# A hybrid attention and convolution layer on eight cores: projection stage reordered with staged weights and dead keys left out, finalize work of a unit spread, tail begun inside the last attention unit

## The chip, the cores and the metric

The kernel runs on all 8 cores of one Trainium2 chip. Times are device microseconds (us) of the slowest core. In the profile, PE is the tensor engine, ACT the ScalarE, DVE the VectorE, POOL the GpSimd and SP the SyncE that issues most loads.

## The reference, cut to what matters

```python
h = rmsnorm(x, mix_norm_g)                       # x: (4, 4096, 1024)
q, k, v, g_attn, cb, cc, ch, g_conv = split(h @ w_in)      # each 512 columns
# A: 4 heads of differential attention with bias -slope_h * |t - s|; slopes 1/4, 1/16, 1/64, 1/256
probs = softmax(q1 k1^T / 8 + bias) - lam * softmax(q2 k2^T / 8 + bias)
o_A   = rmsnorm(probs @ v, subln_g) * (1 - lambda_init) * silu(g_attn)
# B: short gated convolution of width 3
o_B   = cb * conv3(cc * ch) * silu(g_conv)
x = x + concat(o_A, o_B) @ w_out                 # "y" below is this product
gate = sigmoid(rmsnorm(x, ple_norm_g) @ w_ple_gate)
x = x + gate * (p @ w_ple_proj)
return rmsnorm(x, final_norm_g)
```

Each core owns 2048 of the 4096 rows of one sequence (the near half). For attention it also needs k and v of the other 2048 rows (the far half), and computes them itself.

## The kernel before

It has three stages: projections with the gate and the convolution; attention in 16 units (4 heads, 4 query chunks of 512 rows each); and a tail over 16 tiles of 128 rows.

**Projections.** A pipeline normalises 32 row tiles. The k and v weights come by software DMA, which casts them to bf16 on the way. The near half is done in three passes: q with the norm, then k, then v. Every k and q group also has its squares summed over the partitions by one matmul against a matrix of ones, followed by a VectorE maximum. That gives the bound that is subtracted in the exponential.

```python
load_w(0, [(512, 512, 0)])                       # k weights, software DMA with cast
load_w(1, [(1024, 512, 0)])                      # v weights
for s in range(32 + LAG):
    # ... (norm pipelines np_a, np_b; late constants; load of the q weights)
    if 0 <= m < 16:                              # far half
        k_chunk(0, r, j, SO, rdy)                # 8 matmuls of 512 columns
        v_tile(1, 4 * j + r, 16 + 4 * j + r, rdy)
    elif 16 <= m < 32:
        q_chunk(2, r, j, rdy)                    # near half, pass 1
# ...
for tokc in range(4):
    for h in range(NH):
        k_chunk(0, h, tokc, 0, rdy_all)          # near half, pass 2
# ...
for tl in range(16):
    v_tile(1, tl, tl, rdy_all)                   # near half, pass 3
```

**Attention.** For each key tile, two matmuls make the scores, ScalarE takes exponentials of 128x1024 elements, and two tiles later eight matmuls of 129 columns multiply by v. When a group of tiles ends, VectorE moves the accumulators out. When the unit ends, VectorE does the finalize work at once, in one piece:

```python
def finalize_part1(unit, h, qc, tks):            # cut: waits, operands
    reciprocal(rs); tensor_scalar(c2)
    for sb_ in range(4): tensor_scalar(OT[sb_])                 # VectorE
    for sb_ in range(4): scalar_tensor_tensor(OT[sb_])          # VectorE
    tensor_tensor(ON = OT * OT)                                 # VectorE
    tensor_reduce(ssq)                                          # VectorE
    # POOL: variance, power -1/2, ON = OT * rsd
    pending.append([12, part2])                  # transposes and product with the gate, 12 tiles later

for i in range(NT + 2):
    if i < NT: emit_S(i)                         # scores and exponential
    if i >= 2: emit_PV(i - 2)                    # product with v; evacuation; finalize_part1
    # ... run those of pending that have come due
```

**Tail.** The first y tile and 32 fp32 transposes of p follow the last unit, then a barrier, then a loop in stages over the 16 tiles:

```python
for it in range(NTILE + 4):                      # cut: bounds on it
    st_x1n(it - 1)                               # normalise
    st_c2a(it - 2)                               # tanh on ACT, two products on DVE
    st_load(it + 1); st_y(it)                    # 16 matmuls, residual add on DVE
    st_c1(it - 1)                                # transposes, 2 ACT copies, p and gate matmuls
    st_c2b(it - 2); st_sq3(it); st_d(it - 3)     # squares; output
```

Of the kernel before, what the change touches and what calls it, by code (L numbers as in the profile page):

```python
# [18 lines left out]
SLOPES = [2.0 ** (-8.0 * (h + 1) / NH) for h in range(NH)]  # L19
LAMBDA_INIT = 0.8 - 0.6 * 1.0  # L20
# [41 lines left out]
def build_program(debug=None):  # L62
# [6 lines left out]
    p_d = din("p", [SO, 256])  # L69
# [18 lines left out]
    with es:  # L88
# [39 lines left out]
        mx_all = sb("mx_all", [128, 48], F32)  # L128
        negM = sb("negM", [128, 1], F32)
# [17 lines left out]
        mq = sb("mq", [128, 2], F32)  # L147
        mk2 = sb("mk2", [128, 2], F32)
# [26 lines left out]
        for dst, src in [(gmix, gmix_d), (gple, gple_d), (subln, subln_d), (convw, convw_d), (lamv, lam_d)]:  # L175
            tkc = cslot.dma(SP, dst[:], src)
# [5 lines left out]
        POOL.eng.memset(mx_all[:], 0.0)  # L182
# [6 lines left out]
        def late_consts():  # L189
            DVE.need(tkc)  # L190
# [34 lines left out]
        SQB = [cv.take([128, 512], BF16) for _ in range(2)]  # L225
# [16 lines left out]
        with pes:  # L242
# [12 lines left out]
            wslot = [Slot(nc, es, "w%d" % i) for i in range(3)]  # L255
            w_free = [None, None, None]
# [3 lines left out]
            sqb_free = [None, None]  # L260
            mx_idx = [0]
            state = {"xt_free": [None] * NXT, "xn_free": [None, None], "nt": 0, "xt_gen": [0] * NXT,
# [3 lines left out]
            def flush_deferred():  # L266
                while deferred:
                    deferred.pop(0)()
# [9 lines left out]
            class NormPipe:  # L278
# [8 lines left out]
                def _emit_step(self, step):  # L287
# [10 lines left out]
                    if 0 <= i < self.n:  # L298
# [6 lines left out]
                        DVE.need(tk_sq[i])  # L305
                        tk_v[i] = DVE.mark(DVE.eng.tensor_scalar(out=v_all[:, k:k + 1], in0=ss_all[:, k:k + 1],  # L306
# [56 lines left out]
            def norm_bound(s, tk_mm):  # L363
                idx = mx_idx[0]
                mx_idx[0] += 1
                b = idx % 2
                ACT.need(tk_mm, sqb_free[b])
                t_sq = ACT.mark(ACT.eng.activation(out=SQB[b][:], in_=psP[s][:], func=AF.Square))

                def part_b():  # L370
                    PE.need(t_sq, psM_free[0])
                    t_m = PE.mark(PE.eng.matmul(psM[:], lhsT=ones_b[:], rhs=SQB[b][:], start=True, stop=True))  # L372
                    sqb_free[b] = t_m
                    DVE.need(t_m)
                    t_r = DVE.mark(DVE.eng.tensor_reduce(out=mx_all[:, idx:idx + 1], in_=psM[:], axis=AX.X, op=ALU.max))  # L375
                    psM_free[0] = t_r

                deferred.append(part_b)
                return t_sq

            def k_chunk(buf, h, tokc, tokbase, ready_tk):
                s, tk = proj_fm(buf, h * 128, tokc, ready_tk)
                ACT.need(tk)
                t_cp = ACT.mark(ACT.eng.activation(out=KT[:, h, tokbase + tokc * 512: tokbase + (tokc + 1) * 512], in_=psP[s][:],  # L384
                                                   func=AF.Copy))
                t_sq = norm_bound(s, tk)
                psP_free[s] = [t_cp, t_sq]

            def q_chunk(buf, h, tokc, ready_tk):
# [4 lines left out]
                t_sq = norm_bound(s, tk)  # L394
                psP_free[s] = [t_cp, t_sq]

            def v_tile(buf, tl, rglob, ready_tk):
# [3 lines left out]
                for c in range(8):  # L401
                    ins = PE.eng.matmul(psP[s][:], lhsT=HT[:, c, tl * 128:(tl + 1) * 128], rhs=WB[buf][:, c, :],  # L402
                                        start=(c == 0), stop=(c == 7))
                tk = PE.mark(ins)
                flush_deferred()
                DVE.need(tk, tk_pc)
                psP_free[s] = DVE.mark(DVE.eng.tensor_copy(out=VA[:, rglob, :, 0:128],
                                                           in_=psP[s][:].rearrange("p (h d) -> p h d", h=NH)))

            load_w(0, [(512, 512, 0)])  # L410
            load_w(1, [(1024, 512, 0)])
            ht_chunk_free = [None] * 4
            np_a = NormPipe(list(range(16, 32)), lambda i: i * 128, lambda i: None)
            np_b = NormPipe(list(range(0, 16)), lambda i: i * 128, lambda i: ht_chunk_free[i // 4])
            ev0 = np_a.advance(0)
            DVE.need(ev0)
            tk_hth = DVE.mark(DVE.eng.tensor_copy(out=HTH[:], in_=HT[:, :, 0:2]))
            LAG = 4
            for s in range(32 + LAG):
                if s < 16:  # L420
                    np_a.advance(s)
                elif s < 32:
                    np_b.advance(s - 16)
# [5 lines left out]
                if 0 <= m < 16:  # L429
                    j, r = m // 4, m % 4  # L430
                    rdy = np_a.advance(4 * j + 3)
                    k_chunk(0, r, j, SO, rdy)
                    v_tile(1, 4 * j + r, 16 + 4 * j + r, rdy)
                    if r == 3:
                        ht_chunk_free[j] = PE.last()
                elif 16 <= m < 32:
                    j, r = (m - 16) // 4, (m - 16) % 4
                    rdy = np_b.advance(4 * j + 3)
                    q_chunk(2, r, j, rdy)
            flush_deferred()  # L440
            rdy_all = np_b.advance(15)
            norm_done = [state["last_sq"], state["last_xn"], state["last_tr"]]
            w_free[2] = PE.last()
            load_w(2, [(1536, 512, 0)])
            for tokc in range(4):
                for h in range(NH):
                    k_chunk(0, h, tokc, 0, rdy_all)
            flush_deferred()
            w_free[0] = PE.last()
            DVE.need(DVE.last())  # L450
            nq = 16
            nk = 32
            t_a = DVE.mark(DVE.eng.tensor_reduce(out=mq[:, 0:1], in_=mx_all[:, 16:32], axis=AX.X, op=ALU.max))
            DVE.need(t_a)
            DVE.eng.tensor_reduce(out=mk2[:, 0:1], in_=mx_all[:, 0:16], axis=AX.X, op=ALU.max)
            t_b = DVE.mark(DVE.eng.tensor_reduce(out=mk2[:, 1:2], in_=mx_all[:, 32:48], axis=AX.X, op=ALU.max))
            DVE.need(t_b)
            t_c = DVE.mark(DVE.eng.tensor_tensor(out=mq[:, 1:2], in0=mk2[:, 0:1], in1=mk2[:, 1:2], op=ALU.max))
            DVE.need(t_c)
            t_d = DVE.mark(DVE.eng.tensor_tensor(out=mk2[:, 0:1], in0=mq[:, 0:1], in1=mq[:, 1:2], op=ALU.add))  # L460
            DVE.need(t_d)
            tk_negM = DVE.mark(DVE.eng.tensor_scalar(out=negM[:], in0=mk2[:, 0:1], scalar1=-1.0 / 16.0, scalar2=None, op0=ALU.mult))

            DVE.need(tk_negM, LC["t_io"])
            for h in range(NH):
                DVE.eng.tensor_scalar(out=biasA[:, h, :], in0=iotaA[:], scalar1=SLOPES[h], scalar2=negM[:], op0=ALU.mult, op1=ALU.add)
                DVE.mark(DVE.eng.tensor_scalar(out=biasB[:, h, :], in0=(iotaB0 if h == 0 else iotaB)[:], scalar1=-SLOPES[h], scalar2=negM[:], op0=ALU.mult, op1=ALU.add))

            def conv_blocks(cc):
                return [(2048 + cc * 128, 128, 0), (2560 + cc * 128, 128, 128), (3072 + cc * 128, 128, 256),  # L470
                        (3584 + cc * 128, 128, 384)]

            load_w(0, conv_blocks(0))
            for tl in range(16):
                v_tile(1, tl, tl, rdy_all)
            w_free[1] = PE.last()
            load_w(1, conv_blocks(1))
            th_free = [norm_done, norm_done]
            thi = [0]
            for tokc in range(4):  # L480
                for h in range(NH):
# [18 lines left out]
            for cc in range(4):  # L500
# [27 lines left out]
                for tokc in range(4):  # L528
# [16 lines left out]
                    DVE.need(tk_u[min(tokc + 1, 3)], tk_pad, tk_hl, ca_free[a], tkc)  # L545
# [57 lines left out]
        PF32 = rc1.take([128, 16, 256], F32)  # L603
        XT3 = [rc1.take([128, D], F32) for _ in range(2)]
        X1 = [rc1.take([128, D], F32) for _ in range(2)]
# [5 lines left out]
        X1NT = [rc3.take([128, 8, 128], BF16) for _ in range(2)]  # L611
# [14 lines left out]
        ppslot = [Slot(nc, es, "pld%d" % g) for g in range(4)]  # L626
        tk_pld = []
        P3 = {}

        def prefetch_phase3():  # L630
            SP.need(PE.last(), DVE.last())
            gslot.dma(SP, GFIN[:], gfin_d)
            P3["gfin"] = gslot.dma(SP, GPLEB[:], gpleb_d)
            for t_ in range(2):
                P3["ldx", t_] = x3slot[t_].dma(SP, XT3[t_][:], x_d[t_ * 128:(t_ + 1) * 128, :])
            for g in range(4):
                tk_pld.append(ppslot[g].dma(SP, PF32[:, 4 * g:4 * g + 4, :],
                                         p_d.rearrange("(t p) c -> p t c", p=128)[:, 4 * g:4 * g + 4, :]))
# [3 lines left out]
        for half_ in range(2):  # L642
            wt_slot.dma(POOL, WOUT[:, :, half_ * 512:(half_ + 1) * 512],
                        wout_d.rearrange("(c p) n -> p c n", p=128)[:, :, half_ * 512:(half_ + 1) * 512])
        for half_ in range(2):
            wt_slot.dma(POOL, WG[:, :, half_ * 512:(half_ + 1) * 512],
                        wg_d.rearrange("(c p) n -> p c n", p=128)[:, :, half_ * 512:(half_ + 1) * 512])
# [446 lines left out]
```

## Time and profile before

The time before is 963.74 us (median of 3 runs); with one more run on the chip that timed the change, 964.75 us of 4. The profiled execution lasted 961.9 us on its slowest core, core 5.

| stage (median over the 8 cores of the profile) | us |
|---|---|
| start to first projection group | 38.2 |
| start to first exponential (all projections, gate, convolution) | 362.2 |
| units 0 to 3 (head 0) | 56.2 |
| units 4 to 14 | 341.1 |
| unit 15 (the last) | 35.6 |
| last exponential to end (tail) | 164.4 |

I derived the stages from the first exponential of each unit in the trace. The next lines are from the page of the kernel before: part 1 (busy us, share, instructions per engine) and the clock row of part 2 (tenths of full speed, 40 equal slices).

```profile
PE 838.9 (87%) x6210; PEld 445.6 (46%) x6210; DVE 450.7 (47%) x814; ACT 584.3 (61%) x783; POOL 123.5 (13%) x155
...
PEclk9999999999999997888999999999999997999997
```

The tensor engine leads with 87%, but that is an average of stages with different limits. The windows view of core 5 separates them. Its columns are named in its first line: length, then busy us and instructions of each engine, granted clock, DMA share.

```profile
core 5: us, PE busy (x) PEld busy (x) DVE busy (x) ACT busy (x) POOL busy (x), PEclk, DMA share, GB/s
37.00:112.00 75.00, 68.94 (x398) 34.47 (x397) 50.00 (x83) 34.87 (x73) 15.75 (x23) 0.98 0.47 129
112.00:220.00 108.00, 97.06 (x507) 44.91 (x506) 57.38 (x95) 43.47 (x82) 13.71 (x14) 1.00 0.28 49
...
361.00:417.00 56.00, 40.73 (x314) 23.35 (x314) 35.84 (x86) 37.08 (x69) 11.66 (x15) 0.74 0.60 85
...
759.00:795.00 36.00, 32.07 (x335) 19.33 (x332) 8.92 (x23) 33.98 (x36) 2.24 (x3) 1.00 0.01 1
795.00:962.00 167.00, 145.27 (x748) 69.44 (x748) 108.83 (x128) 73.85 (x116) 34.18 (x35) 0.93 0.28 95
```

The far half (37 to 112) and the near half (112 to 220) are tensor work with gaps of 6 and 11 us. Head 0 (361 to 417) has no engine near full and a granted clock of 0.74. In the last unit (759 to 795) ScalarE is busiest with 33.98 us of 36, but the tensor engine follows at 32.07.

The pace of a full tile in that unit stands in the timeline of the tensor engine, core 5 (start us, duration us, engine, line, operation). The last line is from the ScalarE timeline of the same stretch; its bracket is the idle time ahead of it and what ended that.

```profile
769.54 0.37 PE L718 MATMUL psS<-QT,KT 64*128 64x512 bf16 x1
...
769.87 0.63 PE L805 MATMUL psBig<-VA,ARENA 128*128 128x129 bf16 x8
770.55 0.37 PE L718 MATMUL psS<-QT,KT 64*128 64x512 bf16 x1
...
771.88 0.39 PE L718 MATMUL psS<-QT,KT 64*128 64x512 bf16 x1
...
772.77 0.39 PE L718 MATMUL psS<-QT,KT 64*128 64x512 bf16 x1
...
762.25 16.26 ACT L737 ACTIVATE ARENA<-psS,biasB 128x1024 bf16<-128x1024 f32 x16 [0.57 <-PE psS L720]
```

One tile takes 770.55 - 769.54 = 1.01 us, and sixteen exponentials in a row take 16.26 us, 1.02 us each. This is ScalarE's pace. Where the tensor engine had to catch up (starts at 771.88, 772.77 and 773.66 in the same trace) it ran at 0.89 us per tile. So its slack is 1.01 - 0.89 = 0.12 us per tile, not more.

In head 0 the end of a unit looks like this on VectorE (timeline, core 5: start us, duration us, engine, line, operation):

```profile
379.37 0.69 DVE L759 TENSOR_TENSOR ARENA<-ARENA 128x512 f32<-128x512 f32 x1
380.17 0.69 DVE L761 TENSOR_REDUCE ssq<-ARENA 128x4 f32<-128x512 f32 x1
381.03 1.36 DVE L820 TENSOR_TENSOR ARENA<-psBig,fB 128x387 f32<-128x387 f32 x3 [0.17 <-DVE ssq L761]
```

The reduction of the finalize work ends and the next evacuation (L820) follows with 0.17 us of idle time.

In the tail, the chain of waits between 815 and 830 us is tensor work alone. The first line gives shares; each later line is one link: start us, us, what.

```profile
by line: PE psS L900 45.5%; PE psS L950 39.2%; PE psBig L941 11.5%; PE psBig L929 6.0%
...
819.54 3.59 PE psS L950 x16
823.12 3.45 PE psS L900 x16
826.58 0.45 PE psBig L929 x8
827.02 0.86 PE psBig L941 x4
```

L950 is the gate product, L900 the y product, L929 the transposes and L941 the p product. One tile costs about 8.4 us, and the tensor engine waits for nobody.

### The profile page before, as it was taken

The page shows a single profiled execution, that of the slowest core. Times are in us where ns is not written, and L with a number is a line of the kernel's source. Part 1 is how long each engine was busy: PE and PEld are TensorE (multiplying, and loading weights), DVE is VectorE, ACT ScalarE, POOL GpSimd, SP SyncE. Part 2 cuts the span into 40 slices and gives each one's busy share as a digit, 9 for nine tenths or more (in the row PEclk, how much of TensorE's full clock was granted, in tenths as well). Part 3 has the DMA queues.
Part 4 walks back from the last instruction along what each step waited for, and adds up shares of the span by engine and source line. Part 5 has one row for each costly group of instructions (what it writes and reads, how often), then busy time and mean ns, then how long its engine had stood idle before and what let it go on. Part 6 is the DMA issues. An engine that isn't in the chain of part 4 may idle for free.

```text
span 961.9 us, 17031 instructions; the slowest of 8 cores (956.1 to 961.9 us)
## 1 busy us (share of the span) xinstructions
PE 838.9 (87%) x6210; PEld 445.6 (46%) x6210; DVE 450.7 (47%) x814; ACT 584.3 (61%) x783; POOL 123.5 (13%) x155
## 2 busy tenths in 40 slices
PE   0688979999999996889889999899999897999993
PEld 0344434444444443445555555555555554444441
DVE  1577684343277667644432213312312313577775
ACT  2344554502211116779999999999999992455553
POOL 2221130011110002010000000000000001122222
PEclk9999999999999997888999999999999997999997
DMA  8763422055550006700000000000500000133332
GB/s 175 203 154 96 140 73 42 4 44 45 44 44 1 2 1 84 114 1 1 2 2 1 2 2 1 2 1 4 174 1 1 2 1 22 53 124 132 132 110 88
DMA packets 37920, 51.04 MB, mean 53 GB/s; under 512 B 18512, under 2 KB 29392, under 8 KB 37840
## 3 DMA queue, kind: packets, MB, share of 16 engines
q1 hardware_dynamic: 12336, 36.85, 12.0%
q0 software_dynamic: 25504, 13.11, 11.9%
q8 instruction: 52, 0.85, 0.4%
q14 instruction: 28, 0.23, 0.1%
HBM read 54.67 MB, written 8.39 MB: 66 GB/s over the span
## 4 chain that ended last, share of the span: by engine, by line
PE 61%; DVE 13%; ACT 12%; issue 8%; DMA 2%; POOL 2%; DVEq 0%; SPq 0%; ACTq 0%; POOLq 0%
PE psP L357 20%; PE psBig L805 16%; PE psS L718 11%; ACT ARENA L737 8%; PE psP L402 6%; DMA ARENA<-x 2%; PE psS L900 2%; PE psS L950 2%; POOL r L916 2%; DVE VA L961 2%; DVE VA L965 1%; DVE KT L904 1%; ACT SGA L911 1%; DVE psS L728 1%; PE psT L329 1%
## 5 line engine op out<-in xcount | busy, mean ns | idle before, releaser
L737 ACT ACTIVATE ARENA<-psS,biasB 128x1024 bf16<-128x1024 f32 (+3 forms) x292 | 264.2, 1007 | 14.7 <-PE psS L720 13.4
L805 PE MATMUL psBig<-VA,ARENA 128*128 128x129 bf16 x2904 | 254.7, 227 | 16.8 <-DVE ARENA L825 5.8
L357 PE MATMUL psP<-ARENA 128*128 128x512 bf16 x1024 | 232.3, 382 | 0.9 <-DVE ARENA L522 0.7
L805 PEld LDWEIGHTS psBig<-VA,ARENA 128*128 128x128 bf16 x2904 | 173.2, 100 | 110.0 <-issue 101.4
L718 PE MATMUL psS<-QT,KT 64*128 64x512 bf16 (+3 forms) x429 | 152.4, 355 | 35.3 <-ACT ARENA L737 23.7
L720 PE MATMUL psS<-QT,KT 64*128 64x512 bf16 (+3 forms) x429 | 156.4, 365 | 0.0
L357 PEld LDWEIGHTS psP<-ARENA 128*128 128x128 bf16 x1024 | 99.2, 98 | 117.1 <-issue 6.3
L737 ACT ACTIVATE ARENA<-psS,biasA 128x1024 bf16<-128x1024 f32 (+3 forms) x156 | 131.2, 896 | 25.8 <-DVE psS L728 18.1
L718 PEld LDWEIGHTS psS<-QT,KT 64*128 64x128 bf16 x429 | 39.9, 93 | 96.0 <-issue 84.6
L728 DVE SCALAR_TENSOR_TENSOR psS<-T_relu,psS 128x256 f32<-128x256 f32 x64 | 27.4, 427 | 90.9 <-PE psS L720 90.8
L329 PE MATMUL psT<-ident_b,ARENA 128*128 128x128 bf16 x256 | 22.2, 238 | 43.4 <-DVE ARENA L317 21.0
L950 PE MATMUL psS<-ARENA,QT 128*128 128x512 bf16 x256 | 58.4, 381 | 0.0
L402 PE MATMUL psP<-ARENA 128*128 128x512 bf16 x256 | 58.0, 379 | 0.0
L375 DVE TENSOR_REDUCE mx_all<-psM 128x1 f32<-128x512 f32 x48 | 33.1, 690 | 52.4 <-PE psM L372 51.0
L820 DVE TENSOR_TENSOR ARENA<-psBig,fB 128x387 f32<-128x387 f32 (+1 forms) x48 | 22.0, 509 | 67.8 <-PE psBig L805 67.1
L764 POOL TENSOR_SCALAR vsq<-ssq 128x4 f32<-128x4 f32 x16 | 3.1, 192 | 388.7 <-DVE ssq L761 388.7
L384 ACT ACTIVATE KT<-psP 128x512 bf16<-128x512 f32 x32 | 19.1, 596 | 52.0 <-PE psP L357 52.0
L781 DVE SCALAR_TENSOR_TENSOR ARENA<-psBig,sublns,SGA 128x512 bf16<-128x512 f32 x16 | 12.0, 751 | 81.1 <-PE psBig L777 81.1
L309 POOL TENSOR_TENSOR rstd_all<-v_all,mhalf 128x1 f32<-128x1 f32 x32 | 30.8, 964 | 105.5 <-DVE v_all L306 105.4
L825 DVE TENSOR_TENSOR ARENA<-psBig,ARENA 128x387 f32<-128x387 f32 (+1 forms) x48 | 22.3, 510 | 46.8 <-PE psBig L805 46.0
L329 PEld LDWEIGHTS psT<-ident_b,ARENA 128*128 128x128 bf16 x256 | 17.8, 106 | 52.2 <-issue 49.9
L302 ACT ACTIVATE ARENA<-ARENA 128x1024 bf16<-128x1024 f32 x32 | 33.8, 1057 | 10.8 <-DMA ARENA<-x 10.5
(111 smaller groups left out, 875.2 us busy)
## 6 DMA issues: line engine op xcount, KB each, us to landing
ARENA<-x SPq DMA_DIRECT2D x32, 512.0 KB, 3.8
KT<-x SPq DMA_DIRECT2D x16, 512.0 KB, 4.2
y<-VA SPq DMA_DIRECT2D x16, 512.0 KB, 2.9
ARENA<-w_in POOLq DMA_DIRECT2D x4, 1024.0 KB, 17.1
ARENA<-w_in POOLq DMA_DIRECT2D x16, 256.0 KB, 9.1
ARENA<-w_out POOLq DMA_DIRECT2D x2, 1024.0 KB, 13.1
ARENA<-w_g POOLq DMA_DIRECT2D x2, 1024.0 KB, 24.6
KT<-p SPq DMA_DIRECT2D x4, 512.0 KB, 12.4
```

The lines of the kernel that those rows point to most:

```text
L302: tk_sq[i] = ACT.mark(ACT.eng.activation(out=JUNK[:], in_=XT[s][:], func=AF.Square, accum_out=ss_all[:, k:k + 1]))
L309: tk_r[i] = POOL.mark(POOL.eng.tensor_tensor(out=rstd_all[:, k:k + 1], in0=v_all[:, k:k + 1], in1=mhalf[:], op=ALU.pow))
L329: ins = PE.eng.transpose(out=psT[s2][:, c * 128:(c + 1) * 128], in_=XN[s2][:, c * 128:(c + 1) * 128], identity=ident_b[:])
L357: ins = PE.eng.matmul(psP[s][:], lhsT=WB[buf][:, c, wcol0:wcol0 + 128], rhs=HT[:, c, tokc * 512:(tokc + 1) * 512], start=(c == 0), stop=(c ...
L375: t_r = DVE.mark(DVE.eng.tensor_reduce(out=mx_all[:, idx:idx + 1], in_=psM[:], axis=AX.X, op=ALU.max))
L402: ins = PE.eng.matmul(psP[s][:], lhsT=HT[:, c, tl * 128:(tl + 1) * 128], rhs=WB[buf][:, c, :], start=(c == 0), stop=(c == 7))
L718: PE.eng.matmul(psS[b][:, x0:x1], lhsT=KT[0:64, h, kt * 128:(kt + 1) * 128], rhs=QT[0:64, h, qc * 512 + x0:qc * 512 + x1], start=True, sto ...
L720: tk_s = PE.mark(PE.eng.matmul(psS[b][:, 512 + x0:512 + x1], lhsT=KT[64:128, h, kt * 128:(kt + 1) * 128], rhs=QT[64:128, h, qc * 512 + x0: ...
L728: tk_in = DVE.mark(DVE.eng.scalar_tensor_tensor(out=dgb, in0=T_relu[:].unsqueeze(1).to_broadcast([128, 2, 128]), scalar=-2.0 * SLOPES[h], ...
L737: ins = ACT.eng.activation(out=ET[e][:].rearrange("p (j q) -> p j q", j=2)[:, :, s0 * 128:s1 * 128], in_=ps3[:, :, s0 * 128:s1 * 128], fun ...
L805: ins = PE.eng.matmul(acc_region(r), lhsT=ET[e][:, j * 512 + sb_ * 128: j * 512 + (sb_ + 1) * 128], rhs=VA[:, kt, h, :], start=st_, stop=f ...
L950: ins = PE.eng.matmul(psG[:, half_ * 512:(half_ + 1) * 512], lhsT=X1NT[s][:, c, :], rhs=WG[:, c, half_ * 512:(half_ + 1) * 512], start=(c ...
```

## The change

The intent was to feed the tensor engine better in the projections, and to start the tail inside the last unit, where ScalarE sets the pace.

1. The k and v weights come as fp32 over the hardware queue, and ScalarE and GpSimd cast half of each.
2. Far keys whose bias makes the exponential zero are not projected: 4 k groups, and 17 quarters (one head in one tile) of the v tiles.
3. One norm pipeline instead of two. In the near half q, k and v of one chunk follow each other. Half of the v evacuations go to ScalarE, 4 small loads move later.
4. The bound takes four groups at a time: four matmuls of 32 output columns and one maximum instead of four.
5. The finalize work is cut into pieces that run 1, 2, 3, 4, 6 and 12 tiles after the unit, and its square moves to GpSimd.
6. Three y tiles, cut into 24 pieces of two matmuls, run inside the last unit, with their residual adds, squares and normalisation. p arrives transposed from the host. The barrier is gone, and the tail loop has a new order.

The diff holds smaller moves too. The bound is now one per head, and the tables made from it are built between the gate projections. The variance steps of the norms go from VectorE to GpSimd. The weights of the tail come one block at a time at the ends of units, and the last tail tile is handled in halves.

```diff
-load_w(0, [(512, 512, 0)])
-load_w(1, [(1024, 512, 0)])
+def stage_w(buf, c0, stg):                       # 2 loads on SP, fp32
+    # ...
+    def cast():                                  # ACT casts c 0:4, POOL casts c 4:8
+def k_dead(h, j):
+    return SLOPES[h] * (512 * j + 1) >= EXP_ZERO
+def v_h0(tl):
+    return next(h for h in range(NH) if SLOPES[h] * (128 * tl + 1) < EXP_ZERO)
 # ... near half
-        q_chunk(2, r, j, rdy)                    # then all k, then all v
+        for u_ in range(3 * r, 3 * r + 3):
+            if u_ < 4:   q_chunk(2, u_, j, rdy)
+            elif u_ < 8: k_chunk(0, u_ - 4, j, 0, rdy)
+            else:        v_tile(1, 4 * j + u_ - 8, 4 * j + u_ - 8, rdy)
 # ... bound
-    PE.eng.matmul(psM[:], lhsT=ones_b[:], rhs=SQB[b][:], start=True, stop=True)
+    for h in range(NH):
+        src = SQB[grp[h][0]][:] if h in grp else zb
+        PE.eng.matmul(psM[32 * h:32 * h + 32, :], lhsT=ones_b[:, 0:32], rhs=src, start=True, stop=True)
 # ... end of a unit
+for n_, fn in ((1, piece_a), (2, piece_b), (3, piece_c), (4, piece_d), (6, piece_e), (12, piece_f)):
+    pending.append([n_, fn, unit])               # piece_d: square on POOL; piece_e: reduction on DVE
 # ... attention loop
+    if i == first_u15 + 2:
+        for t_ in range(NPRO):                   # NPRO = 3
+            filler += list(y_pieces(t_))
+            if t_ == 0: filler.append(lambda: st_x1n(0))
+            if t_ == 1: filler.append(lambda: st_x1n(1)); filler.append(fill_tr0)
+    if filler: filler.pop(0)()                   # one piece per tile
 # ... tail loop (cut: bounds on it)
+for it in range(NTILE + 1):
+    st_x1n(it + 1)
+    st_g(it)
+    fr["psT3"] = st_tr(it + 1, psT3, fr["psT3"], ACT)   # transposes, two ACT copies
+    st_gate(it, ...)                                    # tanh on ACT, two products on DVE
+    if it < 2:
+        for _ in range(6): run_pending()
+    st_y(it + NPRO); st_sq3(it + NPRO)
+    st_out(it - 1); st_sq4(it)
```

## The prediction

> What bounds it now. The span is 961.9 us, in three stages.
>
> (1) Projections, 0 to about 361 us. The first projection group starts at 37.4 us (timeline); from 5 to 38 us the DMA share is about 1.0 (windows), because two weight casts by software DMA (17.1 us median to landing) share it with x tiles. From there the tensor engine limits: 8 matmuls of 512 columns take 1.73 us (chain of waits). 160 such groups are 277 us, transposes and bound matmuls about 31 us: 308 us of work in 361, so 53 us idle, mostly start-up.
>
> (2) Attention, 361 to 796 us. Exponentials bound heads 2 and 3 (ScalarE 95% busy from 470 us on, 1.14 us for a full tile). Head 0, to 410 us, has ScalarE at 67% and a granted clock of 0.67 to 0.89: VectorE finalize work sits ahead of accumulator evacuations.
>
> (3) Tail, 796 to 962 us. The first gate group starts at 819.5 us, after y tiles, p transposes and a clock of 0.6 to 0.7. Then one 128-row tile per 8.41 us (chain), which is tensor-engine work: 3.45 (y) + 0.86 + 3.45 (gate) + 0.65. The last gate group ends at 950.4 us.
>
> What changes.
> - Weights k and v come as fp32 over the hardware queue and are cast by ScalarE and GpSimd. The Trainium skill ("DMA: Bandwidth & Descriptors", section "Issuing engine by pattern") calls the hardware path generally faster; this trace has no weight load on it. The v cast stands ahead of later norm tiles on ScalarE and GpSimd, so the first groups will stop once for x tile 6. Effective start about 32 us: saves 5.
> - Dead keys: 4 k groups and 4.25 v-tile equivalents vanish: 8.25 x 1.73 = 14 us of tensor work, on the path.
> - Near q, k and v run in one interleaved stream with the norm: about 97 us of work; before, these took 107. With the far half at about 53 us against 75, stage 1 should end near 327 us: saves 34 (the 14 included).
> - Spread finalize: useful only in head 0, about 4 us.
> - Tail: host-transposed p removes 32 fp32 transposes and their copies (8 us of chain). Three y tiles (48 matmuls, 10.4 us) move into the last unit, where a full tile needs about 0.7 us of tensor time (estimate: 0.22 + 8 x 0.06) against 1.14 of ScalarE; so they cost about 3 us there. Gate 0 starts about 2 us after the last exponential instead of 24. Then 13 iterations at 8.4 to 8.9 us: the next tile's two copies stand ahead of the tanh on ScalarE, so the psPP release becomes tight. The last three have no y to hide behind, 6 to 7 us. Tail 143 us against 166: saves 22.
>
> Sum: 34 + 4 - 3 + 22 = 57, so 907 us.
>
> Prediction 907 us, range 890 to 930. Faster by over 2%: 0.96; within 2%: 0.03; slower: 0.01.
>
> Seen right if: first projection group at 24 to 33 us; attention begins at 320 to 332; tensor idle before it below 35 us; last-unit tiles still near 1.15 us; first gate group within 4 us of the last exponential; gate-to-gate 8.4 to 8.9 us.
>
> Wrong if: the fp32 loads starve x, or the casts stall the norm (far half over 65 us); the gate-weight load, issued late, stalls; the y pieces stretch the last unit by over 6 us; the new gate order stalls over 1 us per tile.

## The result, and the profile after

The change made the kernel faster: 932.14 us (median of 4 runs, 931.85 to 932.53) against 964.75 us. The ratio is 0.9662, with a 95% interval of 0.9646 to 0.9679. A ratio is the mean time of one kernel's runs over that of the other's runs of the same rounds, so it is not quite the ratio of the medians. Executions in which one die ran at a lower clock are left out of the means. The profiled run was fast, and its slowest core, core 2, took 931.1 us. The result lies 2 us above the range that was predicted (890 to 930) and 25 us above the middle.

| stage, median of the 8 cores, us | before | after | measured change | predicted change |
|---|---|---|---|---|
| start to first exponential | 362.2 | 323.0 | -39 | -34 |
| head 0 | 56.2 | 57.0 | +1 | -4 |
| units 4 to 14 | 341.1 | 341.0 | 0 | 0 |
| unit 15 | 35.6 | 52.4 | +17 | +3 |
| tail | 164.4 | 155.3 | -9 | -22 |

So the projections gave a little more than predicted, and the other three terms all failed in the same direction. The lines of the page after:

```profile
PE 814.7 (88%) x6148; PEld 431.5 (46%) x6148; DVE 394.0 (42%) x690; ACT 587.0 (63%) x788; POOL 144.1 (15%) x237
...
PEclk9999999999999958889999999999999989899998
```

And the windows of core 2, at the same stages and with the same columns:

```profile
34.00:90.00 56.00, 51.94 (x370) 29.22 (x369) 37.03 (x51) 36.55 (x78) 17.45 (x42) 1.00 0.66 179
90.00:181.00 91.00, 91.00 (x499) 42.25 (x498) 31.39 (x39) 47.52 (x90) 12.04 (x23) 1.00 0.24 49
...
323.00:380.00 57.00, 42.09 (x316) 23.70 (x316) 33.70 (x83) 36.83 (x69) 9.86 (x12) 0.71 0.00 1
...
722.00:776.00 54.00, 45.64 (x385) 23.60 (x386) 15.33 (x32) 38.56 (x41) 5.51 (x10) 0.91 0.09 30
776.00:931.00 155.00, 129.11 (x660) 58.49 (x660) 95.08 (x92) 64.36 (x105) 35.49 (x62) 0.95 0.25 92
```

The near half is now solid tensor work: 91.00 us busy of 91. Head 0 is as long as before, with the clock no better. (The Trainium skill, page "TensorE: Matmul & The Clock Gate", part 1 on the clock gate, states that the clock is at half or full, decided over windows of about 3.4 us of activity. The trace agrees: on core 2 its stretches at half clock last 3.4, 6.8 or 13.7 us, except one of 9.2 us at the very end, and four of them, 34 us together, begin in head 0.) The last unit grew from 36 to 54 us on this core. In the tail the tensor engine has 16 us less to do (145.27 to 129.11), but the stage shrank by less than that.

The last unit, tensor timeline of core 2, for two tiles that carry a filler piece (L951):

```profile
738.48 0.39 PE L797 MATMUL psS<-QT,KT 64*128 64x512 bf16 x1
738.80 0.63 PE L905 MATMUL psBig<-VA,ARENA 128*128 128x129 bf16 x8
739.27 0.59 PE L951 MATMUL psBig<-ARENA,MIXC 128*128 128x512 bf16 x2
739.80 0.39 PE L797 MATMUL psS<-QT,KT 64*128 64x512 bf16 x1
```

A tile now takes 739.80 - 738.48 = 1.32 us instead of 1.01. In it the tensor engine has no gap. The two filler matmuls, 0.216 us each, do not fit into a slack; they stand in line: 0.89 + 2 x 0.216 = 1.32.

Head 0, timelines of GpSimd, VectorE and the tensor engine, core 2 (the bracket is the engine's idle time before the instruction and what ended it):

```profile
355.85 1.04 POOL L847 TENSOR_TENSOR ARENA<-ARENA 128x512 f32<-128x512 f32 x1 [9.24 <-DVE ARENA L840]
356.99 0.69 DVE L851 TENSOR_REDUCE ssq<-ARENA 128x4 f32<-128x512 f32 x1 [1.29 <-POOL ARENA L847]
357.60 1.35 DVE L920 TENSOR_TENSOR ARENA<-psBig,fB 128x387 f32<-128x387 f32 x3
358.29 0.22 PE L905 MATMUL psBig<-VA,ARENA 128*128 128x129 bf16 x1 [1.78 <-DVE ARENA L920]
```

VectorE stands idle for 1.29 us because the reduction (L851) waits for the square, which now runs on GpSimd. Behind the reduction stands the evacuation (L920), and behind that the tensor engine, idle for 1.78 us. Spreading moved the wait; it did not take it away.

The tail, chain of waits from 829 to 840 us, core 2:

```profile
by line: DVE KT L980 22.1%; issue 21.8%; DVE VA L1048 11.2%; DVE QT L999 11.0%; DVE VA L1070 10.8%; ACT ARENA L1012 9.9%; ACT VA L1046 8.4%; PE psBig L1006 5.6%; DVEq L48 1.5%; DVE VA L1051 0.6%; ACTq L48 0.2%
...
829.94 1.22 DVE KT L980
831.16 1.19 DVE VA L1070
832.35 1.21 DVE QT L999
...
833.70 0.62 PE psBig L1006 x8
...
834.40 1.08 ACT ARENA L1012 x2
835.48 0.93 ACT VA L1046
...
836.58 1.23 DVE VA L1048
```

The tensor engine, which was 100% of this chain before, is now 6% of it. The chain is a closed loop: residual add (L980), output (L1070), normalise (L999), transposes (L1006), the two copies (L1012), then the tanh (L1046) of the tile before, its two products (L1048, L1051), and the next residual add at 839.05. One turn is 9.11 us.

The start of the tail on VectorE, core 2:

```profile
788.13 0.87 DVE L834 TENSOR_SCALAR ARENA<-ARENA,c_1 128x128 f32<-128x128 f32 x4
789.11 1.14 DVE L840 SCALAR_TENSOR_TENSOR ARENA<-ARENA,rs 128x128 f32<-128x128 f32 x4
791.60 0.69 DVE L851 TENSOR_REDUCE ssq<-ARENA 128x4 f32<-128x512 f32 x1 [1.35 <-POOL ARENA L847]
792.20 1.21 DVE L980 TENSOR_TENSOR KT<-psS,KT 128x1024 f32<-128x1024 f32 x1
```

The finalize pieces of the last unit stand ahead of the first residual add of the loop (L980). The first two tanh of the tail start at 784.5 and 796.8 us in this trace: 12.3 us apart, not 9.

### The profile page after: what moved, and what is told of

It is laid out like the page before. It is cut to its first block, busy times and chain, and to the rows that moved or that the text cites. A ratio compares the mean times of both kernels' runs of the same rounds, so it can differ in the third digit from the quotient of the medians.

```text
span 931.1 us, 16746 instructions; the slowest of 8 cores (927.2 to 931.1 us)
## 1 busy us (share of the span) xinstructions
PE 814.7 (88%) x6148; PEld 431.5 (46%) x6148; DVE 394.0 (42%) x690; ACT 587.0 (63%) x788; POOL 144.1 (15%) x237
## 3 DMA queue, kind: packets, MB, share of 16 engines
q1 hardware_dynamic: 12192, 38.94, 12.6%
## 4 chain that ended last, share of the span: by engine, by line
PE 56%; DVE 16%; ACT 14%; issue 9%; DMA 3%; POOL 1%; DVEq 0%; SPq 0%; ACTq 0%; POOLq 0%
PE psP L369 18%; PE psBig L905 16%; PE psS L797 11%; ACT ARENA L816 9%; PE psP L425 4%; DMA ARENA<-x 3%; DVE VA L1048 2%; DVE VA L1070 2%; DVE QT L999 2%; ACT ARENA L1012 2%; DVE KT L980 2%; ACT VA L1046 1%; PE psBig L951 1%; DVE psS L807 1%; DVE ARENA L920 1%
## 5 line engine op out<-in xcount | busy, mean ns | idle before, releaser
L369 PE MATMUL psP<-ARENA 128*128 128x512 bf16 x992 | 220.6, 380 | 1.3 <-DVE ARENA L605 1.0
L797 PEld LDWEIGHTS psS<-QT,KT 64*128 64x128 bf16 x429 | 40.0, 93 | 109.4 <-issue 98.8
L847 POOL TENSOR_TENSOR ARENA<-ARENA 128x512 f32<-128x512 f32 x16 | 16.6, 1034 | 429.8 <-DVE ARENA L840 274.2
L1034 PE MATMUL psS<-ARENA 128*128 128x512 bf16 x256 | 57.9, 379 | 2.8 <-ACT VA L1046 2.8
L988 ACT ACTIVATE SGA<-KT 128x1024 bf16<-128x1024 f32 x16 | 16.9, 1057 | 60.7 <-DVE KT L980 58.5
L425 PE MATMUL psP<-ARENA 128*128 128x512 bf16 (+2 forms) x256 | 51.7, 351 | 0.0
L920 DVE TENSOR_TENSOR ARENA<-psBig,fB 128x387 f32<-128x387 f32 (+1 forms) x48 | 21.9, 509 | 60.8 <-PE psBig L905 59.2
L329 DVE TENSOR_SCALAR ARENA<-ARENA,rstd_all 128x1024 bf16<-128x1024 f32 x32 | 24.0, 750 | 48.0 <-POOL rstd_all L321 43.6
L602 ACT ACTIVATE ARENA<-psP 128x512 f32<-128x512 f32 x16 | 9.6, 597 | 49.4 <-PE psP L369 34.5
L1034 PEld LDWEIGHTS psS<-ARENA 128*128 128x128 bf16 x256 | 24.9, 98 | 33.4 <-issue 3.7
L799 PEld LDWEIGHTS psS<-QT,KT 64*128 64x128 bf16 x429 | 40.0, 93 | 0.0
L352 DVE TENSOR_TENSOR ARENA<-psT,gmix_s 128x1024 bf16<-128x1024 bf16 x32 | 39.0, 1218 | 1.3 <-PE psT L341 1.3
## 6 DMA issues: line engine op xcount, KB each, us to landing
QT<-w_in SPq DMA_DIRECT2D x2, 1024.0 KB, 18.6
```

The source lines that it names most:

```text
L329: tk_xn[i] = DVE.mark(DVE.eng.tensor_scalar(out=XN[s2][:], in0=XT[s][:], scalar1=rstd_all[:, k:k + 1], scalar2=None, op0=ALU.mult))
L352: self.ev[i] = DVE.mark(DVE.eng.tensor_tensor(out=HT[:, :, t0_:t0_ + 128], in0=psT[s2][:].rearrange("p (c t) -> p c t", c=8), in1=gmix[:]. ...
L369: ins = PE.eng.matmul(psP[s][:], lhsT=WB[buf][:, c, wcol0:wcol0 + 128], rhs=HT[:, c, tokc * 512:(tokc + 1) * 512], start=(c == 0), stop=(c ...
L425: ins = PE.eng.matmul(psP[s][:, h0 * 128:512], lhsT=HT[:, c, tl * 128:(tl + 1) * 128], rhs=WB[buf][:, c, h0 * 128:512], start=(c == 0), st ...
L797: PE.eng.matmul(psS[b][:, x0:x1], lhsT=KT[0:64, h, kt * 128:(kt + 1) * 128], rhs=QT[0:64, h, qc * 512 + x0:qc * 512 + x1], start=True, sto ...
L799: tk_s = PE.mark(PE.eng.matmul(psS[b][:, 512 + x0:512 + x1], lhsT=KT[64:128, h, kt * 128:(kt + 1) * 128], rhs=QT[64:128, h, qc * 512 + x0: ...
```

## The experiments

Twelve kernels ran; all gave correct results. Each is a small edit of the changed kernel. They ran on three chips, each with its own runs of the kernel before, so times are compared through the ratio to the kernel before. The changed kernel itself stands at 0.9662. One per cent is 9.6 us.

### The y tiles after the unit

```diff
-    for t_ in range(NPRO): filler += list(y_pieces(t_)) ...
-    if filler: filler.pop(0)()
+# after the loop:
+for t_ in range(NPRO):                           # 16 matmuls at once, then add, square, x1n
+    ...
+fill_tr0()
```

> The three y tiles are taken out of the last attention unit and done whole right after it, in two PSUM buffers, with 3.45 us of matmuls each. Theory A (the tensor engine has no slack in that unit: 0.89 us of work per tile against an exponential every 0.89 to 1.0 us): the last unit falls from 54.1 us back to 35 to 37 us, about 12 us come after it, and the whole is 4 to 8 us faster than the changed kernel (932.1 us), so 924 to 928. Rival B (something else in the change lengthened the last unit, such as the spread finalize, the p load or the prefetched x): the last unit stays over 45 us and the whole gets about 10 us slower, 940 or more.

Measured: 928.01 us (3 rounds, one of them slow with 975.37), ratio 0.9629 (0.9613 to 0.9645). Unit 15 went from 52.4 back to 35.8 us, the tail from 155.3 to 168.2. Work done inside the unit cost 16.6 us there and spared 12.9 in the tail. The fill, this change's own idea for the tail, was a small loss: 3 us in the profile and 0.3% in the ratios, whose intervals all but touch (0.9645 and 0.9646). Rival B of the expectation is out, since the unit lost all of its growth with the fill alone.

### Only the matmuls of the fill

```diff
-    st_sq3(t)                                    # inside the last piece of y
+    late.append(lambda: st_sq3(t))               # after the loop
-    filler.append(lambda: st_x1n(0)) ...         # x1n(0), x1n(1), fill_tr0 as fillers
+for fn_ in late: fn_()                           # all after the loop
+st_x1n(0); fill_tr0(); st_x1n(1)
```

> The y matmuls and their residual adds stay in the last unit; the squares on ScalarE, the scaling of the first two tiles on VectorE and the first transpose move behind it. Theory A splits the 18.5 us by which the last unit grew into 10.4 us of matmuls (24 pieces of 0.43) and 8 us of companions that stand ahead of exponentials and accumulator evacuations: the unit falls from 54.1 to 46 to 49 us, and the start of the tail loses 5 to 7 us in exchange, so 930 to 934 us in all. Rival C (the matmuls alone did it, through a lower clock and lost prefetch of weights): the unit stays at 52 us or more, and the whole is 936 or more.

Measured: 931.80 us (3 rounds, one slow with 979.17), ratio 0.9664 (0.9641 to 0.9688). Unit 15 took 45.4 us. So the 48 matmuls and their adds cost 9.8 us in the unit, and the companions another 7.0. The window of the unit on core 2 of this run:

```profile
723.00:769.00 46.00, 41.67 (x377) 21.65 (x379) 12.72 (x29) 36.28 (x37) 3.31 (x5) 1.00 0.11 36
```

The tensor engine's busy time rose from 32.07 us (core 5 of the kernel before) to 41.67, by 9.6, and the unit by about the same amount. The clock was full all the time. The fill's matmuls are 48 x 0.216 = 10.4 us of work, and nearly all of it came on top: the window has 4.3 us of idle tensor time, and the one before had 3.9. The 24 filled tiles at 1.32 instead of 1.01 us explain 7.4 of the 9.8 us. The other 2.4 are not fully separated. The largest single piece in the trace is the tile that also carries the transposes of unit 14's finalize: it takes 3.24 us on core 2, and took 1.33 before (770.55 to 771.88), because the next filler piece uses the same PSUM tile as these transposes and waits 1.0 us for VectorE to empty it.

The other 7 us belong to the companions: squares that stand ahead of exponentials on ScalarE, and normalisations that stand ahead of evacuations on VectorE. The waits view of the changed kernel's last unit (core 2) has 4.0 us of tensor idle time that ended with ScalarE, in four waits, the longest 1.8 us, and 1.5 us that ended with one evacuation. The clock has a share too: the changed kernel has 3.4 us at half clock in this unit on six cores and 10.2 us on cores 2 and 5, and this run has none on any core. At half speed, 3.4 us cost at most 1.7, so on most cores the waits are the larger part. Taking the companions out of the unit did not save time in all, since they then stood in the tail (157.9 us).

### The tanh ahead of the copies

```diff
     st_g(it)
     if it + 1 < NTILE:
+        st_tanh(it)
         fr["psT3"] = st_tr(it + 1, psT3, fr["psT3"], ACT)
     st_gate(it, ...)                             # uses the tanh if it is there already
```

> In the tail, ScalarE does the tanh of tile t before the two copies of the transposed tile t+1, nothing else moved. Theory D (the 9.11 us of one tail tile is a closed loop: copies, tanh, five VectorE operations of 1.22 us, transposes): the loop opens and a tile takes the 8.4 us of its tensor work, 12 tiles times 0.7, so 922 to 926 us. Rival E (VectorE or the output stores set the 9.11 us): a tile stays at 9.0 us or more and the whole within 2 us of 932.

Measured: 917.53 us (3 rounds), ratio 0.9531 (0.9511 to 0.9552). The tail went from 155.3 to 139.2 us. Its chain from 829 to 842 us, core 5:

```profile
by line: PE psS L1034 53.1%; PE psS L951 29.9%; PE psBig L1024 13.3%; PE psBig L1006 5.6%
```

It is all tensor work again, at 8.21 us per tile (gate products start at 830.09 and 838.30). The closed loop is open, because the tanh no longer waits for copies that themselves wait for the normalisation of a later tile. One instruction moved on an in-order engine was worth 12.6 us. The Trainium skill, page "Perfetto Trace Analysis", section "Tensor Engine Instruction (MATMUL, LD_WEIGHTS)", says "ACT/DVE/GPSIMD are strict FIFO". This run agrees: no arithmetic changed, and the chain lost its VectorE and ScalarE links.

### The last finalize before the tail loop

```diff
+for _ in range(6): run_pending()
 for it in range(NTILE + 1):
     ...
-    if it < 2:
+    if it == 1:
         for _ in range(6): run_pending()
```

> The last unit's finalize pieces up to the sum of squares are issued before the first gate group and not after the first gate, on engines that are idle then. Theory F (they stood ahead of the residual add of tile 3 on VectorE, one of them waiting for GpSimd, so the tensor engine idled and its clock halved): the time from the first gate group to the third falls from 23.6 us by 5 to 8, so 924 to 927 us. Rival G (that stretch is bound by the loop of 9.1 us per tile and the half clock anyway): gain under 2 us.

Measured: 928.97 us (3 rounds, one slow with 990.55), ratio 0.9640 (0.9624 to 0.9656). The tail is 149.7 us, 5.6 less. The first two tanh start at 786.6 and 795.2 us, 8.6 us apart instead of 12.3. So the finalize pieces in front of the residual add cost about 5 us of the tail in the profile, and 2 us in the timed runs, where the intervals overlap. (In the profile of this run the first exponential comes 1.2 us later than in that of the changed kernel, so the whole span shows less than the tail does.)

### The reduction of the finalize two tiles later

```diff
-(4, piece_d), (6, piece_e), (12, piece_f)
+(4, piece_d), (8, piece_e), (12, piece_f)
```

> One piece of the spread finalize, the VectorE reduction that waits for a GpSimd multiply, is issued two tiles later, so that it stands behind the first-group accumulator evacuation of head 0's next unit and not ahead of it. Theory H (the spread gained nothing in head 0 because it only exchanged one head-of-line wait on VectorE for another: 1.29 us idle plus 0.69 of reduction ahead of the evacuation, tensor engine idle 1.78 us): units 0 to 3 take 51 to 54 us together against 57.1 now, the whole 926 to 930 us. Rival I (head 0 is bound by the evacuations, the diagonal corrections and the half clock themselves): units 0 to 3 stay at 55.5 or more and the whole within 1.5 us of 932.

Measured: 935.28 us (5 rounds), ratio 0.9696 (0.9674 to 0.9718). That is no gain at all. But the stages show two opposite things: head 0 fell from 57.0 to 51.3 us, and the tail rose from 155.3 to 161.7. The tail calls the pending pieces six times per tile, which no longer reaches a count of 8, so the last unit's finalize came one tile later. The next run takes it out.

### The same, with the tail's count kept

```diff
-    for _ in range(6): run_pending()
+    for _ in range(8 if it == 0 else 6): run_pending()
```

> As reduce_later (the waiting reduction two tiles later), but with the tail's first batch of finalize pieces long enough to hold the later piece, which reduce_later had pushed one tail tile back: there head 0 fell from 57.0 to 51.3 us (median of the cores) and the tail grew from 155.3 to 161.7. Theory H with that repair: head 0 at 50 to 53 us, the tail at 154 to 156, the whole 926 to 928 us. Rival (the gain in head 0 is given back later by whatever grew the tail): the tail again over 160 and the whole within 2 us of 932.

Measured: 928.81 us (5 rounds, one slow with 979.84), ratio 0.9641 (0.9619 to 0.9662). Head 0 is 51.8 us, the tail 154.6, the profiled median span 923.5 against 928.7 us. In the ratios the gain is 2 us, and the intervals overlap. The VectorE timeline of core 2 in head 0:

```profile
343.22 0.89 DVE L920 TENSOR_TENSOR ARENA<-psBig,fB 128x387 f32<-128x387 f32 x2 [0.31 <-PE psBig L905]
344.03 0.42 DVE L807 SCALAR_TENSOR_TENSOR psS<-T_relu,psS 128x256 f32<-128x256 f32 x1
344.36 0.68 DVE L851 TENSOR_REDUCE ssq<-ARENA 128x4 f32<-128x512 f32 x1
```

The evacuation now comes first, and the reduction finds its input ready. This shows that the order on VectorE, and not the amount of work, held head 0 at 57 us. The half-clock time inside head 0 fell with it, from 31.4 to 25.6 us (medians of the cores). But the clock is the smaller part. On core 2 the half-clock time did not fall (33.6 and 37.0 us), and its head 0 still went from 57.0 to 53.7 us; the cores with 17.1 us of half clock reach 49.7.

### The finalize in one piece again

```diff
-((1, piece_a), (2, piece_b), (3, piece_c), (4, piece_d), (6, piece_e), (12, piece_f))
+((1, piece_a), (1, piece_b), (1, piece_c), (1, piece_d), (1, piece_e), (12, piece_f))
 def piece_d():
-    tk["on"] = POOL.mark(POOL.eng.tensor_tensor(...))
+    tk["on"] = DVE.mark(DVE.eng.tensor_tensor(...))
```

> The finalize of every unit is issued in one go right after its last evacuation, its multiply back on VectorE, as before the change; only its transpose stays 12 tiles later. If the spread was worth the 4 us that I predicted, head 0 takes 60 us or more instead of 57.1 and the whole 935 or more. If it was worth nothing (theory H or I), head 0 stays within 1.5 us of 57 and the whole within 2 us of 932.

Measured: 925.12 us (5 rounds), ratio 0.9598 (0.9571 to 0.9624). It is not quite the old code, since the pieces run one tile after the unit. Head 0 is 56.0 us and the tail 150.1. Part 5 of the change, as it was made, cost about 6 us: nothing gained in head 0 and some 5 us lost in the tail. The tail here is as short as with the last finalize before the loop (149.7 us), so the loss there is the late place of the last unit's pieces. The intervals of the two ratios do not overlap.

### All keys projected

```diff
 def k_dead(h, j):
-    return SLOPES[h] * (512 * j + 1) >= EXP_ZERO
+    return False
 def v_h0(tl):
-    return next(h for h in range(NH) if SLOPES[h] * (128 * tl + 1) < EXP_ZERO)
+    return 0
```

> The skip of dead keys is undone: all 16 k groups and all 16 v tiles of the far half are computed in full. Theory (tensor work on the path): 4 k groups and 4.25 v equivalents at 1.73 us, so stage 1 ends 13 to 15 us later and the whole is 945 to 948 us. Rival (the far half waits for x anyway, so the skipped work was partly idle time): 5 to 10 us, so 937 to 942.

Measured: 942.46 us (3 rounds), ratio 0.9774 (0.9748 to 0.9800). The first exponential comes at 333.0 instead of 323.0 us, all of it in the far half (first q copy at 101.4 instead of 91.5). The dead keys are worth 10 us. Their tensor work is 8.25 x 1.73 = 14 us, as predicted. That only 10 of 14 count is seen in the traces: from the first projection group to the first q copy, the tensor engine idles 0.4 us with all keys projected and 4.1 us without the dead ones (medians of the cores). Some of the freed time became waiting, which is nearer the rival of the expectation than its theory.

### The weights by software DMA again

```diff
+load_w(0, [(512, 512, 0)])
+load_w(1, [(1024, 512, 0)])
-    cast_k = stage_w(0, 512, QTF[:]); cast_k()
-    cast_v = stage_w(1, 1024, SGAF[:])
-    cast_v()
```

> The k and v weights come again by the casting software queue at the start, nothing else undone. Theory as predicted (the hardware queue with casts is worth about 5 us): the first projection group starts at 37 to 40 us instead of 32 to 34 and the whole is 935 to 938. Rival (the bytes bound the start whichever queue moves them): within 2 us of 932.

Measured: 930.17 us (3 rounds), ratio 0.9645 (0.9620 to 0.9670). The first projection group starts at 31.1 us instead of 32.7, and the first exponential comes 1.5 us earlier. Its tensor timeline, core 0 of that run, and then a GpSimd line of the changed kernel, core 2:

```profile
32.04 4.42 PE L369 MATMUL psP<-ARENA 128*128 128x512 bf16 x10 [5.38 <-DMA ARENA<-w_in]
```

```profile
25.86 1.89 POOL L447 CAST ARENA<-QT 128x2048 bf16<-128x2048 f32 x1 [11.08 <-DMA QT<-w_in]
```

So the staged weights bought nothing, and cost 1.5 us in the profile; the timed difference is inside the interval. It was not that they came late: with staging the k weights lay cast in SBUF at 26.9 us and the v weights at 34.8, against 30.9 and 41.0 us here (medians of the cores). But the casts of k stand ahead of later norm steps on two in-order engines: ScalarE idles 6.5 us and GpSimd 10.6 us (medians) until the load lands. x tile 5 lands later as well: its square starts at 25.8 us on core 5, here at 20.5. So the first projection group waits behind the transposes of x tiles 4 and 5. Here those tiles are ready, and the group waits for the weights instead. No run separates the two or tries another place for the casts. The start came forward from 38.2 us with either path. The rest of the change did that; one part that the trace shows is that the x loads begin at 1.07 us instead of 3.38, since four small loads moved behind them.

### The bound at full width

```diff
-t_m = PE.eng.matmul(psM[32 * h:32 * h + 32, :], lhsT=ones_b[:, 0:32], rhs=src, start=True, stop=True)
+t_m = PE.eng.matmul(psM[:], lhsT=sel_b[:, h, :], rhs=src, start=(h == 0), stop=(h == NH - 1))
```

`sel_b[:, h, :]` is zero but for ones in columns 32h to 32h+31, so the result is the same.

> The four 32-column bound matmuls of a group become four accumulating 128-column ones with a block of ones each, same count, same result. Theory J (the four 32-column ones ran beside each other: a group holds the tensor engine 0.333 us in the trace, against 0.216 for each single one before; I had called the count unchanged and expected nothing): 12 groups take 0.86 us instead, stage 1 ends 5 to 7 us later and the whole is 936 to 939 us. Rival K (they are off the path): within 2 us of 932.

Measured: 936.25 us (3 rounds), ratio 0.9726 (0.9704 to 0.9748). The first exponential comes at 327.4 us, 4.4 later. First the tensor timeline of the changed kernel (core 2), then of this one (core 0): the four bound matmuls and the start of what follows them.

```profile
49.05 0.40 PE L395 MATMUL psM<-ARENA,ones_b 128*32 128x512 bf16 x4
49.38 0.99 PE L425 MATMUL psP<-ARENA 128*128 128x384 bf16 x5
```

```profile
49.80 1.03 PE L399 MATMUL psM<-ARENA,MIXC 128*128 128x512 bf16 x4
50.66 1.14 PE L429 MATMUL psP<-ARENA 128*128 128x384 bf16 x6
```

Four narrow matmuls hold the engine for 0.33 us, four wide ones for 0.86: the narrow ones overlap. Twelve such groups make 6.4 us of tensor time, of which 4.4 arrived.

### The near half in three passes again

```diff
-for u_ in range(3 * r, 3 * r + 3): ...           # q, k, v of one chunk
+q_chunk(2, r, j, rdy)                            # then all k, then all v
```

> Only the interleaving in the near half is undone: q alone runs beside the norm of the near tiles, then k, then v, as before the change. Theory L (interleaving keeps the tensor engine fed while the norm supplies one tile in about 2 us): the near half, 90.8 us now, takes 100 to 106, the whole 941 to 947 us. Rival M (the gaps of before came from the restart of a second norm pipe and from VectorE and the bound matmuls, which stay changed): near half below 95 us, the whole under 937.

Measured: 936.48 us (3 rounds), ratio 0.9722 (0.9700 to 0.9745). The first exponential comes at 328.7 us. The interleaving is worth 5.7 us. From the first q copy to the last copy of the near half's q, k and v it takes 96.2 us, against 89.7 in the changed kernel and 106.1 before, and the tensor engine idles 4.8, 0.0 and 10.8 us there (medians of the cores). So the order is less than half of what the near half gained. The whole stayed under 937 us, as rival M of the expectation had it, but the near half not under its 95.

### All repairs together

The y tiles after the unit, the tanh ahead of the copies, the reduction two tiles later, the last finalize before the loop (with eight calls), and the weights by software DMA.

```diff
+load_w(0, ...); load_w(1, ...)                   # and stage_w gone
-(6, piece_e)
+(8, piece_e)
-    if filler: filler.pop(0)()
+for t_ in range(NPRO): ...                       # y tiles after the unit
+for _ in range(8): run_pending()
 for it in range(NTILE + 1):
     st_g(it)
+    st_tanh(it)
     st_tr(it + 1, ...)
-    if it < 2:
+    if it == 1:
```

> The repairs together: y tiles after the last unit, tanh before the copies, the reduction later, the last finalize early, and the weights by the software queue. By stages (median of the cores, now): stage 1 323.1 to 321.5, head 0 57.0 to 51.5, the last unit 52.5 to 36, the tail 155.3 plus 12.5 for the y tiles less 16 for the loop less 3 for the finalize, so 149. Sum about 900 us; 896 to 906 if the gains add, over 908 if two of them were the same wait.

Measured: 903.09 us (3 rounds, 901.46 to 903.49), ratio 0.9375 (0.9354 to 0.9396). It beats both kernels: 2.9 points below the changed kernel, some 28 us. The stages are 320.9, 51.4, 341.9, 35.6 and 147.9 us. The single repairs' gains, 3.2, 12.6, 2.1, 2.0 and 1.6 us from the ratios, add up to 21.5, each uncertain by about 2 us. The repairs do not hinder each other, within these uncertainties.

## Why the prediction was right or wrong

It was right that the change is faster by over 2%, and wrong in the size: -57 us predicted, -33 measured. The steps, as the prediction put them:

- **"Three y tiles ... where a full tile needs about 0.7 us of tensor time (estimate: 0.22 + 8 x 0.06) against 1.14 of ScalarE; so they cost about 3 us there."** This step failed most: 16.6 us. Both numbers were wrong, and the trace of before had better ones. The tensor engine runs at 0.89 us per tile when it catches up, ScalarE at 1.02. So the slack is 0.12 x 35 tiles = 4 us for 10.4 us of matmuls, and a filled tile takes 1.32 us. The windows row said the same: 32.07 us busy of 36. At that pace the pair of score matmuls takes 0.33 us to the next instruction (771.88 to 772.21) and the eight of 129 columns 0.56 us (772.21 to 772.77), where the estimate had 0.22 and 0.48. ScalarE's 1.14 us was one record's length, which overlaps the next. With the matmuls alone the unit grew by 9.8 us; the companions added 7, which the prediction had not counted at all. Its own condition for being wrong, "the y pieces stretch the last unit by over 6 us", came true.

- **"Tail 143 us against 166: saves 22."** Measured 155.3 against 164.4. Two terms were mis-sized. (a) "13 iterations at 8.4 to 8.9 us" were 9.11 in the chain. The prediction saw the copies ahead of the tanh and called the release of one buffer tight. It did not follow the ring further, from tanh through the VectorE products and the normalisation back to the copies. Breaking the ring brought 8.21 us per tile and a tail of 139.2. (b) The start: the last unit's finalize in front of the first residual add, 5.6 us of tail. "First gate group within 4 us of the last exponential" was right: last exponential at 775.8, gate group at 779.3 on core 2.

- **"Spread finalize: useful only in head 0, about 4 us."** Measured +1 us there and a loss of 5 in the tail. The prediction saw rightly that VectorE work sits ahead of evacuations, but it did not check that piece_e, six tiles later, falls just before the next evacuation, with a GpSimd instruction of 1.04 us in front of it. Two tiles later the gain is 5 us.

- **"Stage 1 should end near 327 us: saves 34."** Measured 323.0, -39; the sum was nearly right by luck, for its parts were not. The staged weights, "saves 5", cost 1.5, because the casts of k, and an x tile that landed later, held the norm; the prediction had named the cast of v alone. The start still came near its 32 us (32.7), but not through the weights. The dead keys, 14, gave 10. The interleaving gave 5.7, the narrow bound matmuls 4.4, which the prediction had as nothing. These four make 18.6 of 39. The other 20 us lie with what I did not undo alone: the single norm pipeline and the order of the far half, 36 fewer VectorE maxima (0.69 us each), v evacuations half on ScalarE, and the earlier x loads. By stretch about 7 of them are in the start, 8 in the far half and 6 in the near half, less 1 in the gate and convolution after it. How they divide among these edits stays open.

The terms close: relative to the prediction, 14 us lie in the last unit, 13 in the tail and 5 in head 0, less 5 from the projections. That is 27, against a miss of 25.

## What to carry to other kernels

Before you fill an engine's slack, read that slack from the pace of the stage and from its busy time in that window, not from the lengths of single records: here about 4 us were free, 10.4 were put in, and the unit grew by 9.8. Before you reorder a loop across in-order engines, follow each wait around until it closes; one ScalarE instruction behind two copies made a ring of 9.1 us out of 8.2 us of tensor work. Work that is spread over later tiles, or that waits for a load, must be placed against the next thing that its engine has to do in time. And when only the sum of a prediction is right, undo the parts one by one before believing any of them.

## What the Trainium skill lacked or had wrong

- "DMA: Bandwidth & Descriptors", section "Issuing engine by pattern", calls the hardware path generally faster than the software one. The prediction leaned on that. By the hardware queue, casts included, the k and v weights were ready at 26.9 and 34.8 us, by the casting software queue at 30.9 and 41.0 (other traffic and the order of the loads differed too). The same page's "Rules for kernel authors" sends a transfer that casts to GpSimd, the software path. What is lacking is the price of the other way: here each cast took 1.9 us, and ScalarE and GpSimd idled 6.5 and 10.6 us in front of the first ones, and the first projection group started 1.6 us later (32.7 against 31.1).
- "TensorEngine Tiling (Array Packing)", section "Theoretical Speedup", gives "Up to 4×" for a small dimension of at most 32. Four bound matmuls of 32 output columns held the engine for 0.33 us against 0.86 us at full width: 2.6 times. The page has no measured figure. "TensorE: Matmul & The Clock Gate", part 3, has one for three column tiles and none for four.
- "Perfetto Trace Analysis", section "Optimization Strategy", advises to interleave stages that are limited by different engines. It tells how to find gaps on the engine that one optimises for, but not how to measure the room on the one that is to take the extra work. Here it was 4 us in a unit of 35.6, and interleaving cost 16.6 us to spare 12.9.
